# A hybrid token mixer on one core: the first recurrent phase rewritten with channels on partitions

## The chip, the cores and the metric

One core of a Trainium2 chip runs the whole program once. The metric is device time in microseconds (us), from the profiler's first to last event; lower is better. The engines are TensorE (PE, with its weight loads as PEld), VectorE (DVE), ScalarE (ACT), GpSimd (POOL) and SyncE (SP), which issues most DMAs.

## The reference, cut to what matters

Two layers of a mixer over 256 context and 1024 latent tokens of width 1024. Each layer projects the normed tokens and runs four groups of heads: a gated long convolution, a bidirectional RWKV-7 recurrence, windowed attention and dense attention. The change is in the recurrence:

```python
kk = heads(k * k_k); kk = kk / max(norm(kk), 1e-12)
for d in range(2):                       # forward and backward
    w_log = -softplus(-(w0[d] + tanh(w_low) @ w_up[d])) - 0.5
    a = sigmoid(a0[d] + a_low @ a_up[d])
    k_d = k * (1 + (a - 1) * k_a)
    w = exp(-exp(w_log))
# per token: S = S * w + (S @ -kk) (kk * a)^T + v k_d^T ;  y = S @ r
bonus = sum(r * (k_fwd + k_bwd) * r_k) * v
```

There are four heads of 64 channels. The kernel computes the recurrence in chunks of 64 tokens: within a chunk the products of decayed keys, queries and removal vectors form triangular Gram matrices, which are inverted by blocks.

## The kernel before, in words

Everything is fp32; the large projections run as three fp32r products (high and low halves of tokens and weights). Instructions are written in program order, and a planner fixes each engine's queue ahead of time: an instruction goes to its engine when its operands are expected and no earlier one is ready. `nc.any` lets the planner choose VectorE or ScalarE.

**Projections.** `chan` (L240 to L249) computes 128 output channels, in groups of 24 matmuls, into one of three PSUM banks `acc`; `conv` (L251) copies a group into `zp`, which has one buffer, and applies a three-tap convolution (L261 to L263). `attn` (L301) uses the same tag `acc`. `beside` (L284) adds the projections that other stages need; `spread` and `mark` tie each group to a point in TensorE's order, here to the ends of the first eight of ten tiles (PACE_A is 0 to 0.8).

**The first recurrent phase**, `phase_a` (L449), takes ten tiles of 128 tokens. `stage_a` (L481) loads r, k, v and the low-rank rows with channels on partitions (L484 to L489), computes the decays (`p_w`, L491), transposes r, k and v to tokens on partitions (`p_rk`, `p_v`), and forms sigmoid rates, cumulative decays (`p_ex`, `p_in`, L520, triangular fp32r matmuls over high and low halves), the chunk's total decay (`p_wt`, L532), normed keys (L535 to L544), and the operands AL, BK and rho (L546 to L560), all token-major and on VectorE. Then sixteen transposes (L576 to L579) bring them back to channels on partitions as AR and BKT, and sixteen matmuls give the Gram matrices `p_g` (L594), which VectorE masks into GG (L597). Blocks of GG are copied into cL and cN (L607, L610) and stored to `ls_d` and `no_d`; `p_r` (L619) closes the tile, and the mark is set there. Copies by `cpy` all carry line L456.

**The solves.** After tiles 4, 8 and 10, `solve` (L624) loads the 32x32 blocks (L631), copies them into Lx, the upper half reversed, and inverts them in 31 steps of two VectorE operations each (L641, L642); the result is copied (L644) and stored from ScalarE's queue (L645, L646). All its tiles have one buffer.

**After it.** The projections of two more gate blocks are tied behind the last tile; then the long convolution (`hyena`) begins, then the second recurrent phase (`phase_b`), which reads what the first one stored, beside the attentions.

PSUM in this stretch: `acc` 3 banks, tag a 2, tag g 3.

Of the kernel before, what the change touches and what calls it, by code (L numbers as in the profile page):

```python
# [7 lines left out]
F32 = mybir.dt.float32  # L8
F32R = mybir.dt.float32r
# [206 lines left out]
class Proj:  # L216
# [18 lines left out]
    def chan(w, blk, ctx, pace=None):  # L235
# [64 lines left out]
    def attn(w, sa, pq):  # L300
# [20 lines left out]
        for a, blk in ((0, B_WA), (1, B_FA)):  # L321
# [4 lines left out]
            for half in range(2):  # L326
# [8 lines left out]
                for t in (list(range(8)) + ([8, 9] if half or not w.last else [])):  # L335
                    lat = t < 8
                    ps = pp.tile([128, 512], F32, tag="acc", bufs=3, name="acc")
# [73 lines left out]
def rw_consts(c):  # L411
# [6 lines left out]
    c["cind"] = (((s // 64)[:, None] == np.arange(2)[None, :]).astype(f) * f(NE))  # L418
# [7 lines left out]
class Rwkv:  # L426
# [7 lines left out]
    def __init__(w, k, l, keep, dp):  # L434
# [10 lines left out]
        w.ls_d = [T(f"ls_d{i}_", [2, m, 4, 4, 32, 32]) for i, m in enumerate(w.NBAT)]  # L445
# [3 lines left out]
    def phase_a(w, ep, sp, pp):  # L449
# [5 lines left out]
        PT = nc.gpsimd.tensor_tensor  # L455
        cpy = lambda o, i: nc.any.tensor_copy(o, i)  # L456
        vcp = cpy
        ld = lambda n, shape, src: (lambda t: (nc.scalar.dma_start(out=t, in_=src), t)[1])(ep.tile(shape, F32, name=n))
        tri = ep.tile([128, 4, 128], F32R, name="trir")
        t = ep.tile([128, 4, 128], F32, tag="zb", bufs=2, name="tri")  # L460
        nc.scalar.dma_start(out=t, in_=A["tri"])
        nc.any.tensor_copy(tri, t)
        rv = ld("rvec", [128, 3, 256], A["rvec"][l, :, 0:3])
        cind = ld("cind", [128, 2], A["cind"])
        gmask = ld("gmask", [128, 2, 2, 64], A["gmask"])
        wup = ld("wup", [65, 512], A["wup"][l])
        aup = ld("aup", [65, 512], A["aup"][l])
        LW = [ep.tile([65, 2, 128], F32, name=f"LW{i}") for i in range(2)]
        for i in range(2):
            nc.sync.dma_start(out=LW[i][64:65], in_=A["ones"][0:2].rearrange("(o a) c -> o a c", o=1))  # L470
        W2, W1 = 7, 5
        w2 = lambda n, shape=(128, 2, 256): sp.tile(list(shape), F32, tag="w2", bufs=W2, name=n)
        w1 = lambda n, shape=(128, 256): sp.tile(list(shape), F32, tag="w1", bufs=W1, name=n)
        pa = lambda n, shape=(128, 512): pp.tile(list(shape), F32, tag="a", bufs=2, name=n)
        pg_ = lambda n, shape=(128, 512): pp.tile(list(shape), F32, tag="g", bufs=3, name=n)
        d2 = lambda x: x.unsqueeze(1).to_broadcast([128, 2, 256])
        h4 = lambda x: x.rearrange("p (h d) -> p h d", d=64)
        half = lambda c: slice(c * 64, c * 64 + 64)

        def stage_a(b, n):  # L480
            t0 = b * 128  # L481
            zb = ep.tile([128, 8, 128], F32, tag="zb", bufs=2, name="zb")
            q = nc.sync if n else nc.scalar
            q.dma_start(out=zb[:, 0:6, :], in_=k.rw_d[0:768, t0:t0 + 128].rearrange("(c p) t -> p c t", p=128))  # L484
            for c in range(2):
                q.dma_start(out=zb[:, 6:8, half(c)],
                                  in_=k.rw_d[512:768, t0 + (1 - c) * 64:t0 + (2 - c) * 64].rearrange("(c p) t -> p c t", p=128))
            lw = LW[n % 2]
            q.dma_start(out=lw[0:64], in_=k.rw_d[768:896, t0:t0 + 128].rearrange("(c p) t -> p c t", p=64))  # L489
            ps = pa("p_w")  # L490
            nc.tensor.matmul(ps, lw[:, 0, :], wup, start=True, stop=True)  # L491
            sig = w2("sig")
            nc.scalar.activation(sig, ps, AF.Tanh, scale=0.5)
            nc.any.tensor_scalar(sig, sig, 0.5, 0.5, op0=ALU.mult, op1=ALU.add)
            p0 = pa("p_rk", (128, 4, 128))
            for i in range(4):
                nc.tensor.transpose(p0[:, i, :], zb[:, i, :], k.ident)
            rk = w2("rk")
            cpy(rk, p0)
            r_, k_ = rk[:, 0, :], rk[:, 1, :]  # L500
            p1 = pa("p_v", (128, 4, 128))
            for i in range(4):
                nc.tensor.transpose(p1[:, i, :], zb[:, 4 + i, :], k.ident)
# [4 lines left out]
            ps = pa("p_a")  # L508
            nc.tensor.matmul(ps, lw[:, 1, :], aup, start=True, stop=True)
            ta = w2("ta")  # L510
            nc.scalar.activation(ta, ps, AF.Tanh, scale=0.5)
            ss = [sp.tile([128, 2, 256], F32R, tag=f"ss{i}", bufs=1, name=f"ss{i}") for i in range(2)]
            nc.any.tensor_copy(ss[0], sig)
            TT(ss[1], sig, ss[0].bitcast(F32), op=ALU.subtract)
            E = []
            for nm, kinds in (("ex", (0, 2)), ("in", (1, 3))):
                ps = pa("p_" + nm, (128, 2, 256))
                for d in range(2):
                    for i, x in enumerate(ss):
                        nc.tensor.matmul(ps[:, d, :], tri[:, kinds[d], :], x[:, d, :], start=(i == 0), stop=(i == 1))  # L520
                e = w2("e" + nm)
                nc.scalar.activation(e, ps, AF.Exp, scale=NE)
                E.append(e)
                if nm == "in":
                    e = w2("en")
                    nc.scalar.activation(e, ps, AF.Exp, scale=-NE)
                    E.append(e)
            E1, E3, E2 = E
            ps = pa("p_wt", (128, 2, 2, 2))
            for d in range(2):  # L530
                for hp in range(2):
                    nc.tensor.matmul(ps[:, d, :, hp], sig[:, d, hp * 128:(hp + 1) * 128], cind, start=True, stop=True)  # L532
            nc.scalar.activation(w.WT[:, b], ps.rearrange("p d c h -> p (d c h)"), AF.Exp)
            kkr = w1("kkr")
            TT(kkr, k_, rv[:, 0, :], op=ALU.mult)  # L535
            sq = w1("sq")
            nc.scalar.activation(sq, kkr, AF.Square)
            ss = sp.tile([128, 4], F32, tag="ss", bufs=2, name="ss")
            nc.vector.tensor_reduce(ss, h4(sq), axis=AX.X, op=ALU.add)
            nc.vector.tensor_scalar(ss, ss, 1e-24, None, op0=ALU.max)  # L540
            s2 = sp.tile([128, 4], F32, tag="s2", bufs=2, name="s2")
            PT(s2, ss, k.mhalf[:, :4], op=ALU.pow)
            kkh = w1("kkh")
            STT(h4(kkh), h4(kkr), 0.5, s2.unsqueeze(2).to_broadcast([128, 4, 64]), op0=ALU.mult, op1=ALU.mult)  # L544
            AL = sp.tile([128, 2, 2, 256], F32, tag="AL", bufs=2, name="AL")
            STT(AL[:, 0], E1, -2.0, d2(kkh), op0=ALU.mult, op1=ALU.mult)  # L546
            kka = w2("kka")
            STT(kka, ta, 1.0, d2(kkh), op0=ALU.add, op1=ALU.mult)
            kxa = w1("kxa")
            STT(kxa, k_, 0.5, rv[:, 1, :], op0=ALU.mult, op1=ALU.mult)  # L550
            kd = w2("kd")
            STT(kd, ta, -1.0, d2(kxa), op0=ALU.add, op1=ALU.mult)
            TT(kd, kd, d2(k_), op=ALU.add)
            rho = w2("rho")
            BK = sp.tile([128, 2, 2, 256], F32, tag="BK", bufs=2, name="BK")
            for c in range(2):
                q, z = half(c), half(1 - c)
# [1094 lines left out]
```

## Time and profile before

| | |
|---|---|
| three runs, median (lowest, highest) | 2539.47 us (2528.05, 2540.99) |
| the profiled execution, its time | 2539.31 us |
| its span, first to last instruction | 2537.5 us |
| busy: PE, PEld, DVE, ACT, POOL | 2231.6, 1844.7, 1740.8, 1079.7, 270.0 us |
| mean granted TensorE clock | 0.926 of 2.4 GHz |
| DMA | 359.07 MB, mean 142 GB/s |

The busy times overlap; no engine is full over the whole span, and the stages have different limits. A busy TensorE is not a TensorE at its peak, since matmuls are pipelined.

### The profile page before, as it was taken

What the parts mean: (1) busy time and instruction counts of PE and PEld (TensorE: products, weight loads), DVE (VectorE), ACT (ScalarE), POOL (GpSimd) and SP (SyncE); (2) the same over time, 40 slices, a digit from 0 to 9 for tenths busy, and PEclk for the clock granted to TensorE, in tenths of its full rate; (3) what the DMA queues carried; (4) which work ended last, traced back from release to release, by engine and by line L of the source; (5) the groups of instructions that cost most, each with busy time, mean ns of one, the idle gap of its engine ahead of it and who ended that gap; (6) DMA issues with size and microseconds to landing.
All of it is one profiled execution on the core that took longest, in us unless ns stands there. A gap on an engine that the chain in (4) does not pass through costs nothing.

```text
span 2537.5 us, 44541 instructions
## 1 busy us (share of the span) xinstructions
PE 2231.6 (88%) x16864; PEld 1844.7 (73%) x16864; DVE 1740.8 (69%) x4146; ACT 1079.7 (43%) x2564; POOL 270.0 (11%) x404
## 2 busy tenths in 40 slices
PE   6899898998948699999798998989987669999898
PEld 3687677777847577886586887978776557877676
DVE  6985445789778666667543786657997886656753
ACT  5422222544211366766544322335542107766651
POOL 1000221000000001002122001310000000001212
PEclk9899899899778799999998998999987879999999
DMA  8224574556422746443433222444655155563332
GB/s 266 75 102 162 185 229 108 155 171 201 158 86 79 230 117 183 146 144 89 141 124 117 94 90 95 133 125 142 179 177 169 67 137 169 173 202 94 120 129 100
DMA packets 288690, 359.07 MB, mean 142 GB/s; under 512 B 108007, under 2 KB 229910, under 8 KB 283100
## 3 DMA queue, kind: packets, MB, share of 16 engines
q1 hardware_dynamic: 261704, 261.60, 33.3%
q0 software_dynamic: 11232, 70.78, 8.2%
q10 hardware_dynamic: 15540, 23.84, 2.9%
q8 instruction: 133, 2.18, 0.4%
q14 instruction: 81, 0.66, 0.1%
HBM read 227.31 MB, written 128.84 MB: 140 GB/s over the span
## 4 chain that ended last, share of the span: by engine, by line
PE 68%; DVE 11%; DMA 9%; ACT 5%; issue 5%; SPq 1%; POOL 0%; ACTq 0%; POOLq 0%; DVEq 0%
PE acc L246 20%; PE acc L340 9%; PE ops L1112 8%; PE O L1014 3%; PE pt L1004 3%; DMA st_d<-ST 2%; PE p_g L594 2%; PE pk L1326 2%; PE S L973 2%; ACT P L988 1%; PE pr L1387 1%; PE mps L130 1%; PE S L974 1%; PE ph L1302 1%; DVE tmp L641 1%
## 5 line engine op out<-in xcount | busy, mean ns | idle before, releaser
L246 PE MATMUL acc<-hhi,wh 128*128 128x512 f32 (+1 forms) x896 | 219.8, 383 | 7.8 <-ACT wh L232 5.2
L246 PE MATMUL acc<-hlo,wh 128*128 128x512 f32 (+1 forms) x896 | 213.7, 373 | 0.0
L246 PE MATMUL acc<-hhi,wl 128*128 128x512 f32 (+1 forms) x896 | 211.0, 371 | 1.5 <-DVE wl L233 1.5
L978 DVE TENSOR_REDUCE st<-S 128x1 f32<-128x512 f32 (+1 forms) x320 | 172.1, 560 | 55.9 <-PE S L974 40.0
L988 ACT ACTIVATE P<-S,st 128x512 f32<-128x512 f32 (+1 forms) x320 | 183.9, 585 | 24.2 <-DVE st L981 21.7
L246 PEld LDWEIGHTS acc<-hhi,wh 128*128 128x128 f32 x896 | 159.0, 198 | 40.0 <-ACT wh L232 7.2
L246 PEld LDWEIGHTS acc<-hhi,wl 128*128 128x128 f32 x896 | 155.2, 190 | 32.6 <-issue 5.8
L246 PEld LDWEIGHTS acc<-hlo,wh 128*128 128x128 f32 x896 | 157.1, 193 | 28.0 <-issue 2.0
L944 ACT COPY PT<-pt 128x512 f32<-128x512 f32 (+2 forms) x284 | 133.4, 497 | 91.5 <-PE pt L1004 89.7
L1004 PE MATMUL pt<-ident,P 128*128 128x128 f32 x976 | 158.8, 286 | 13.6 <-ACT P L988 6.2
L973 PE MATMUL S<-kp,qs 128*128 128x256 f32 (+2 forms) x384 | 141.4, 377 | 23.8 <-ACT P L988 23.1
L1004 PEld LDWEIGHTS pt<-ident,P 128*128 128x128 f32 x976 | 113.4, 144 | 43.3 <-issue 15.2
L1014 PE MATMUL O<-PT,V 128*64 128x256 f32 x976 | 133.2, 386 | 1.8 <-ACT PT L944 1.8
L974 PE MATMUL S<-kp,qs 128*128 128x256 f32 (+2 forms) x384 | 120.4, 327 | 1.3 <-DMA kp<-qk_d 1.3
L232 ACT ACTIVATE wh<-wr 128x1024 fp32r<-128x1024 f32 x58 | 60.7, 1057 | 116.9 <-PE acc L246 88.6
L973 PEld LDWEIGHTS S<-kp,qs 128*128 128x128 f32 x384 | 75.4, 197 | 42.4 <-ACT P L988 30.8
L1014 PEld LDWEIGHTS O<-PT,V 128*64 128x64 f32 x976 | 70.9, 136 | 42.5 <-issue 5.2
L340 PE MATMUL acc<-wh,hhi 128*128 128x256 f32 x608 | 93.3, 296 | 2.0 <-ACT wh L232 2.0
L258 ACT COPY zp<-acc 128x512 f32<-128x512 f32 (+1 forms) x64 | 33.6, 531 | 143.4 <-PE acc L246 109.1
L340 PE MATMUL acc<-wl,hhi 128*128 128x256 f32 x608 | 90.5, 289 | 4.1 <-POOL wl L233 4.1
L594 PEld LDWEIGHTS p_g<-AR,BKT 64*128 64x128 f32 x640 | 72.0, 209 | 27.1 <-ACT BKT L456 8.8
L345 ACT ACTIVATE qx<-acc 128x256 f32<-128x256 f32 x76 | 29.2, 384 | 137.9 <-PE acc L340 136.7
(397 smaller groups left out, 5290.8 us busy)
## 6 DMA issues: line engine op xcount, KB each, us to landing
IN<-in_d POOLq DMA_DIRECT2D x18, 2048.0 KB, 10.0
wr<-in_w_in POOLq DMA_DIRECT2D x58, 512.0 KB, 4.3
mw<-in_mod_w SPq DMA_DIRECT2D x48, 512.0 KB
in_d<-BK SPq DMA_DIRECT2D x20, 512.0 KB
in_d<-AL SPq DMA_DIRECT2D x20, 512.0 KB
kp<-qk_d SPq DMA_DIRECT2D x32, 320.0 KB
qk_d<-qo SPq DMA_DIRECT2D x72, 128.0 KB
in_d<-GG SPq DMA_DIRECT2D x18, 512.0 KB
```

The lines of the kernel that those rows point to most:

```text
L232: w.k.nc.scalar.activation(h, r, AF.Copy)
L246: nc.tensor.matmul(ps[:, :n], a[:, kc * 128:(kc + 1) * 128], b[:, kc, t0:t0 + n], start=(i == 0 and kc == 0), stop=(i == 2 and kc == 7))
L340: nc.tensor.matmul(ps[:, :256], x_[:, kc, t * 128:(t + 1) * 128], w_[:, kc, :], start=(n == 0 and kc == 0), stop=(n == 2 and kc == 7))
L594: nc.tensor.matmul(pg[:, hp, c], BKT[q, hp, c], AR[q, :, hp, half(c)], start=True, stop=True)
L944: nc.any.tensor_copy(o, i)
L973: nc.tensor.matmul(ps[:, w0:w0 + w], qs[:, hd % 2, hd // 2], kp[kv][0][:, t0:t0 + w], start=True, stop=False)
L974: nc.tensor.matmul(ps[:, w0:w0 + w], qs[:, hd % 2, hd // 2], kp[kv][1][:, t0:t0 + w], start=False, stop=not masks)
L978: TR(ng[:, i:i + 1], ps[:, :w0], axis=AX.X, op=ALU.max, negate=True)
L988: nc.scalar.activation(P[:, :w], ps[:, :w], AF.Exp, bias=gm, accum_out=den[:, i:i + 1])
L1004: nc.tensor.transpose(pt[:, i, :], P[:, i * 128:(i + 1) * 128], k.ident)
L1014: nc.tensor.matmul(O[kv * 64:kv * 64 + 64, 0], V[:, t, kv * 64:kv * 64 + 64], PTs[kv][:, i], start=(i == 0), stop=(i == nt - 1))
L1112: nc.tensor.matmul(ps, a[:, kc, :], b[:, kc, s], start=(n == 0 and kc == 0), stop=(n == 2 and kc == 7))
```

## The change

Work stays with channels on partitions as long as it can. `stage_a` is split in two. `early` loads k, the low-rank rows, r and v, squares the keys and sums them by a matmul with head indicators (`p_n`), computes the decays and rates, forms all cumulative decays at once with channels on partitions (`p_e`: the sigmoid is the stationary operand, the triangular matrices move, in fp32), takes the chunk's total decay out of that result, and spreads the key norms over channels by a matmul with a broadcast operand. `products` forms AR and BKT directly, takes the Gram matrices, stores blocks straight from GG (eight stores instead of three), makes the token-major copies AL and BK by twelve transposes, and computes the bonus sums by matmuls (`p_bon`). `early` of tile n+1 is written ahead of `products` of tile n. The solve loads its blocks tile by tile and direction by direction, without the copy into Lx's lower half. The tag `acc` has two PSUM banks, as `p_n` takes one. The rest of the diff (layout of the constants, one line in `phase_b`) follows from this and is left out.

```diff
-            ps = w.pp.tile([128, 512], F32, tag="acc", bufs=3, name="acc")
+            ps = w.pp.tile([128, 512], F32, tag="acc", bufs=2, name="acc")
...
-        def stage_a(b, n):
+        def early(b, n):
+            t0 = b * 128
             q = nc.sync if n else nc.scalar
+            X = ep.tile([128, 2, 3, 128], F32, tag="X3", bufs=2, name="X3")
+            q.dma_start(out=X[:, :, 0], in_=rows(256, 256, slice(t0, t0 + 128)))
             lw = LW[n % 2]
             q.dma_start(out=lw[0:64], in_=k.rw_d[768:896, t0:t0 + 128].rearrange("(c p) t -> p c t", p=64))
+            q.dma_start(out=X[:, :, 2], in_=rows(0, 256, slice(t0, t0 + 128)))
+            zv = ep.tile([128, 4, 128], F32, tag="zv", bufs=1, name="zv")
+            q.dma_start(out=zv[:, 0:2], in_=rows(512, 256, slice(t0, t0 + 128)))
+            for c in range(2):
+                q.dma_start(out=zv[:, 2:4, half(c)], in_=rows(512, 256, slice(t0 + (1 - c) * 64, t0 + (2 - c) * 64)))
+            for p in range(2):
+                ACT(sq[:, p], X[:, p, 0], AF.Square, scale=rv[:, 0, p:p + 1])
+            pn = pp.tile([128, 3, 128], F32, tag="n", bufs=1, name="p_n")
+            for p in range(2):
+                nc.tensor.matmul(pn[:, 2, 2 * p:2 * p + 2], sq[:, p], ind, start=True, stop=True)
...
+            ACT(ta, ps, AF.Tanh, scale=0.5)
+            KK = w4("KK")
+            nc.any.tensor_scalar(KK[:, :, :, 1].rearrange("q p d t -> q (p d) t"), pd(ta), -0.5, -0.5, op0=ALU.mult, op1=ALU.add)
+            for p in range(2):
+                ACT(KK[:, p, :, 0], ta[:, p], AF.Identity, scale=cf[:, 1, p:p + 1], bias=cf[:, 2, p:p + 1])
...
+            for p in range(2):
+                ps = pa("p_e", (128, 2, 2, 128))
+                for d in range(2):
+                    c0 = d * 256 + p * 128
+                    nc.tensor.matmul(ps[:, d], sig[:, c0:c0 + 128], tri[:, 2 * d:2 * d + 2], start=True, stop=True)
+                ACT(AR[:, p], ps, AF.Exp, scale=NE)
+                ACT(E2[:, p], ps[:, :, 1], AF.Exp, scale=-NE)
...
+            for h in range(4):
+                nc.tensor.matmul(pn[half(h % 2), h // 2], s2[:, h:h + 1].to_broadcast([128, 64]), k.ident, start=True, stop=True)
+            for p in range(2):
+                STT(X[:, p, 1], X[:, p, 0], cf[:, 0, p:p + 1], pn[:, p], op0=ALU.mult, op1=ALU.mult)
+            return X, KK, AR, E2, VV
+
+        def products(b, X, KK, AR, E2, VV):
+            TT(at(KK), at(KK), two(0), op=ALU.mult)
+            BKT = w4("BKT", (128, 2, 2, 2, 2, 64))
+            for c in range(2):
+                x = KK.rearrange("q p d a t -> q (p d) a t")[:, :, :, half(c)]
+                TT(BKT.rearrange("q p d c a t -> q (p d) c a t")[:, :, c], x if c else x[:, :, ::-1],
+                   pd(E2)[:, :, half(c)].unsqueeze(2).to_broadcast([128, 4, 2, 64]), op=ALU.mult)
+            TT(at(AR), at(AR), two(1), op=ALU.mult)
+            if need_y:
...
+                TT(M, KK[:, :, :, 0], X[:, :, 2:3].to_broadcast([128, 2, 2, 128]), op=ALU.mult)
...
             for c in range(2):
                 for hf in range(2):
-                    p = c * 64 + hf * 32
-                    cpy(cL[p:p + 32], Gu[p:p + 32, :, c, hf * 32:hf * 32 + 32])
+                    e = c * 2 + hf
+                    o = slice(32 * e, 32 * e + 32)
+                    nc.sync.dma_start(out=w.ls_d[i][m].rearrange("d u e s t -> e s (d u) t")[e], in_=Gu[o, :, c, hf * 32:hf * 32 + 32])
...
+                    nc.sync.dma_start(out=w.no_d[b][o].rearrange("p (u t) -> p u t", t=32), in_=Gu[o, 4 * d:4 * d + 4, c, x:x + 32])
...
+                for p in range(2):
+                    for d in range(2):
+                        nc.tensor.matmul(ps[:, 2 * p:2 * p + 2], M[:, p, d], rki[:, p], start=(d == 0), stop=(d == 1))
+                cpy(w.bon[:, b, :], ps)
...
-            nc.sync.dma_start(out=Ld[:P], in_=flat(w.ls_d[i]))
...
-            cpy(Lx[lo], Ld[lo])
+            for m in range(w.NBAT[i]):
+                for d, t in ((1, Ld), (0, Lx)):
+                    o = 16 * (d * w.NBAT[i] + m)
+                    nc.sync.dma_start(out=t[o:o + 16].rearrange("p s t -> p (s t)"), in_=rows(w.ls_d[i], d)[m])
...
+        nxt = early(w.ORDER[0], 0)
         for n, b in enumerate(w.ORDER):
-            stage_a(b, n)
+            cur = nxt
+            if n < 9:
+                nxt = early(w.ORDER[n + 1], n + 1)
+            products(b, *cur)
             if n in (3, 7, 9):
                 solve(n // 4)
             yield
```

## Rows read from the trace of the kernel before

**Rows 1.** Busy time by stretch, both layers (window, length, engines, granted clock, DMA share).

```profile
468.10:624.20 156.10, 152.47 (x1122) 125.41 (x1120) 136.92 (x287) 74.45 (x147) 10.89 (x20) 1.00 0.59 175
624.20:664.10 39.90, 30.14 (x206) 25.25 (x200) 36.38 (x86) 15.07 (x33) 1.01 (x1) 0.64 0.41 121
664.10:717.00 52.90, 33.60 (x190) 29.50 (x188) 38.18 (x104) 8.29 (x15) 1.12 (x2) 0.82 0.58 191
...
1730.80:1875.20 144.40, 142.40 (x1004) 113.59 (x1000) 129.23 (x272) 73.79 (x146) 9.61 (x19) 0.98 0.57 173
1875.20:1917.00 41.80, 30.70 (x204) 24.51 (x199) 39.40 (x97) 14.26 (x31) 2.03 (x2) 0.66 0.41 124
```

**Rows 2.** Waits, 664 to 717 us: who waited for whom, total, times, longest.

```profile
ACT u L1372 <- DVE XR L644: 17.5, 1, 17.5
```

**Rows 3.** Groups of VectorE instructions, 434.5 to 666.5 us: busy and mean ns, idle before.

```profile
L559 DVE TENSOR_TENSOR BK<-kd,en 64x512 f32<-64x512 f32 x20 | 13.7, 686 | 0.6
...
L233 DVE TENSOR_TENSOR wl<-wr,wh 128x1024 fp32r<-128x1024 f32 x6 | 7.3, 1219 | 0.1
L553 DVE TENSOR_TENSOR kd<-kd,rk 128x512 f32<-128x512 f32 x10 | 6.9, 689 | 0.2
...
L456 DVE COPY cN<-GG 32x128 f32<-32x128 f32 x22 | 4.9, 221 | 0.5
...
L564 DVE TENSOR_TENSOR bs<-kd 128x256 f32<-128x256 f32 x10 | 4.3, 426 | 0.3
```

**Rows 4.** Chain of waits at full clock, 1740 to 1800 us (start, us, what).

```profile
1746.31 0.67 PE p_ex L520 x4
1746.98 0.47 PE p_in L520 x4
...
1752.48 0.79 PE p_wt L532 x8
...
1753.44 0.86 PE p_w L491 x2
...
1758.04 0.44 PE p_rk L497 x4
```

**Rows 5.** Timeline of the first tile of layer 0 (start, length, engine, line).

```profile
435.38 5.03 ACTq L486 DMA_DIRECT2D zb<-rw_d  x2
...
440.45 0.65 ACTq L489 DMA_DIRECT2D LW<-rw_d  x1
...
445.08 2.07 PE L491 MATMUL p_w<-wup,LW 65*128 65x512 f32 x2 [9.62 <-DMA LW<-rw_d]
...
460.83 2.60 PE L594 MATMUL p_g<-AR,BKT 64*128 64x128 f32 x24
```

**Rows 6.** Busy time, pairs of tiles in layer 1 with equal projection work.

```profile
1730.80:1770.70 39.90, 39.73 (x296) 32.14 (x292) 29.96 (x56) 20.75 (x43) 2.83 (x7) 1.00 0.43 139
1770.70:1815.80 45.10, 43.68 (x304) 34.24 (x301) 41.02 (x85) 25.21 (x49) 3.54 (x8) 0.97 0.64 192
...
1833.90:1875.20 41.30, 41.14 (x297) 32.91 (x292) 40.42 (x94) 20.42 (x41) 3.22 (x4) 1.00 0.65 196
```

**Rows 7.** VectorE timeline, 618 to 722 us: the second and third solve.

```profile
633.42 0.69 DVE L634 COPY Lx<-Ld 64x1024 f32<-64x1024 f32 x1 [2.18 <-DMA Ld<-ls_d]
...
677.62 0.69 DVE L644 COPY XR<-X 64x1024 f32<-64x1024 f32 x1
...
690.26 0.18 DVE L641 TENSOR_TENSOR tmp<-Lx,X 64x31 f32<-64x31 f32 x1 [0.40 <-ACT Lx L456]
...
715.31 0.68 DVE L644 COPY XR<-X 32x1024 f32<-32x1024 f32 x1
```

**Rows 8.** Timeline of the rw projections of layer 0, 173 us.

```profile
173.28 2.10 PE L246 MATMUL acc<-hhi,wh 128*128 128x512 f32 x8
...
173.37 0.86 ACT L258 COPY zp<-acc 128x256 f32<-128x256 f32 x2 [6.33 <-PE acc L246]
```

**Rows 9.** Instructions on ls_d, whole span: duration ns min/median/max, first and last start.

```profile
L612 SPq DMA_DIRECT2D ls_d<-cL x40: 373/530/1822, 471.0 to 1919.2; - x40
```

More of the change, by code (lines that the diff above doesn't have):

```diff
@@ L483, in stage_a @@
             q = nc.sync if n else nc.scalar
[L484 to L487, printed above, removed]
+            rows = lambda r, m, s: k.rw_d[r:r + m, s].rearrange("(c p) t -> p c t", p=128)
+            X = ep.tile([128, 2, 3, 128], F32, tag="X3", bufs=2, name="X3")
@@ L496, in stage_a @@
[L496 to L500, printed above, removed]
+            ps = pa("p_a", (128, 2, 2, 128))
+            for p in range(2):
+                for d in range(2):
+                    c0 = d * 256 + p * 128
+                    nc.tensor.matmul(ps[:, p, d], aup[:, c0:c0 + 128], lw[:, 1, :], start=True, stop=True)
+            ta = w2("ta")
+            ACT(ta, ps, AF.Tanh, scale=0.5)
@@ L528, in stage_a @@
[L528 to L555, printed above, removed]
@@ L556, in stage_a @@
-            for c in range(2):
-                q, z = half(c), half(1 - c)
-                TT(BK[q, c], kka[q], E2[q], op=ALU.mult)
-                TT(BK[z, c], kd[q], E2[q], op=ALU.mult)
-            TT(rho, E3, d2(r_), op=ALU.mult)
-            nc.sync.dma_start(out=w.bk_d[b], in_=BK)
-            if not (last and b >= 8):
-                bs = w1("bs")
-                TT(bs, kd[:, 0, :], kd[:, 1, :], op=ALU.add)
-                TT(bs, bs, r_, op=ALU.mult)
-                TT(bs, bs, rv[:, 2, :], op=ALU.mult)
-                nc.vector.tensor_reduce(w.bon[:, b, :], h4(bs), axis=AX.X, op=ALU.add)
+            AR = w4("AR")
@@ L568, in stage_a @@
             GG = sp.tile([128, 2, 2, 2, 2, 2, 64], F32, tag="GG", bufs=1, name="GG")
             GA, GR = GG[:, :, :, :, :, 0], GG[:, :, :, :, :, 1]
-            ops = []
             for d in range(2):
-                p0 = pg_("p_ar", (128, 2, 2, 128))
-                p1 = pg_("p_bk", (128, 2, 2, 128))
-                for hp in range(2):
-                    sl = slice(hp * 128, hp * 128 + 128)
-                    nc.tensor.transpose(p0[:, 0, hp, :], AL[:, 0, d, sl], k.ident)
-                    nc.tensor.transpose(p0[:, 1, hp, :], rho[:, d, sl], k.ident)
-                    for c in range(2):
-                        nc.tensor.transpose(p1[:, hp, c, :], BK[:, c, d, sl], k.ident)
-                AR = w2("AR", (128, 2, 2, 128))
-                cpy(AR, p0)
-                if not (last and b >= 8):
-                    nc.sync.dma_start(out=w.rh_d[b][:, 256 * d:256 * d + 256], in_=AR[:, 1])
-                BKT = w2("BKT", (128, 2, 2, 128))
-                cpy(BKT, p1)
-                ops.append((AR, BKT))
@@ L587, in stage_a @@
-            for d in range(2):
-                AR, BKT = ops[d]
                 for par in range(2):
                     pg = pg_("p_g", (128, 2, 2, 2, 64))
-                    q = half(par)
-                    for hp in range(2):
+                    o = half(par)
+                    for p in range(2):
                         for c in range(2):
-                            nc.tensor.matmul(pg[:, hp, c], BKT[q, hp, c], AR[q, :, hp, half(c)], start=True, stop=True)
-                    z = 1 if last and b >= 8 else 2
+                            nc.tensor.matmul(pg[:, p, c], BKT[o, p, d, c], AR[o, p, d, :, half(c)], start=True, stop=True)
@@ new lines, in products @@
+            AL = sp.tile([128, 2, 2, 256], F32, tag="o4", bufs=2, name="AL")
+            p0 = pg_("p_al", (128, 2, 2, 128))
+            for d in range(2):
+                for p in range(2):
+                    nc.tensor.transpose(p0[:, d, p], AR[:, p, d, 0], k.ident)
+            cpy(AL[:, 0], p0.rearrange("t d p e -> t d (p e)"))
+            BK = sp.tile([128, 2, 2, 256], F32, tag="o4", bufs=2, name="BK")
+            for c in range(2):
+                p0 = pg_("p_bk", (128, 2, 2, 128))
+                for d in range(2):
+                    for p in range(2):
+                        nc.tensor.transpose(p0[:, d, p], BKT[:, p, d, c].rearrange("q a t -> q (a t)"), k.ident)
+                cpy(BK[:, c], p0.rearrange("t d p e -> t d (p e)"))
@@ L614, in stage_a @@
+            nc.sync.dma_start(out=w.bk_d[b], in_=BK)
+            if need_y:
+                ps = pg_("p_bon", (128, 4))
+                for p in range(2):
+                    for d in range(2):
+                        nc.tensor.matmul(ps[:, 2 * p:2 * p + 2], M[:, p, d], rki[:, p], start=(d == 0), stop=(d == 1))
+                cpy(w.bon[:, b, :], ps)
             pr = pg_("p_r", (128, 2, 4, 64))
```

99 lines of the change are left out of this document (46 added, 53 removed).

## The prediction, made blind

> **What bounds the kernel now.** I read the busy time by stretch first, then the chain of waits, then the groups of instructions inside the phase, and last the timelines of its two ends. The change touches the first recurrent phase of each layer: about 230 us in layer 0 (434 to 664 us) and 220 us in layer 1 (1698 to 1917 us), 18% of the 2537.5 us span together.
>
> In its body, from the last matmul of the first token tile to that of the eighth, TensorE is busy 152.5 of 156.1 us at the full granted clock, 2.4 GHz, and VectorE 136.9 us; in layer 1 142.4 and 129.2 of 144.4 us [rows 1]. Both engines are nearly full, because the other projections are fed in between. In the tail (the last two tiles) no projection is left: VectorE is busy 36.4 of 39.9 us and 39.4 of 41.8 us, TensorE 30 us, at a mean granted clock of 0.64 and 0.66, so between its two levels [rows 1]. The tail is VectorE's, since the second 32x32 solve runs there beside the tiles. Then a third solve, VectorE alone, must finish before the long convolution starts: ScalarE waits 17.5 us for its last copy [rows 2]. So three things set the start of the next stage: the first tile's latency, TensorE in the body, and VectorE's tile work mixed into the second solve.
>
> Durations come from the profiled execution, 2539.31 us for a span of 2537.5 us; the median of the three runs shown is 2539.47 us, so the sum can be set against either.
>
> **Part 1, VectorE and ScalarE.** With channels on partitions, per-channel factors become scalars of an instruction, and products with r, k and the keys run once for both directions. Gone per tile from VectorE: six operations on 512 elements (low half of the sigmoid, kka, AL, two on kd, rho) at 0.69 us, four 64-partition products at 0.686 us, eight operations of 256 elements at 0.42 us, and VectorE's share of the copies into cL and cN, some 1.0 us a tile [rows 3]: 4.1 + 2.7 + 3.4 + 1.0 = 11.2 us. Added: two products of 1024 elements at 1.22 us, three of 512 at 0.69 us (two for BKT, one for M) and two of 128 elements, which I put at 0.3 us each, under the 0.42 us of 256 elements [rows 3]: 5.1 us. Net 6 us less per tile. ScalarE loses casts and copies and gains two exponentials of 256 elements; it is busy 74 of 156 us [rows 1], so I cost it at nothing. If that cover went, 2 us a tile would show.
>
> **Part 2, TensorE.** At the full clock a 512-column fp32 matmul of two weight halves costs 0.86 us, a two-column one 0.79/4 = 0.20 us, a transpose 0.11 us, and the eight fp32r matmuls of the cumulative sums 1.14 us [rows 4]. Added per tile: the cumulative sums as four fp32 matmuls of 256 columns, 4 x 0.43 = 1.72 us; two norm sums, 0.40 us; four broadcasts of 128 columns, 4 x 0.215 = 0.86 us; four bonus sums, 0.79 us. Gone: 1.14 us, the decay sums 0.79 us, four r and k transposes 0.44 us, four of the eight AL and rho transposes 0.44 us. Net +0.96 us. Over the eight tiles up to the tail that is **+8 us** a layer if TensorE is the limit. Here the row (busy 98%) speaks for the whole price; the lower end is 0. I take 8.
>
> The Trainium skill, page "Trainium Kernel Development and Optimization", section "Performance Expectations", calls matmul busy time a bad measure because matmuls are pipelined, and goes by weight-load busy time. That is 125.4 of 156.1 us, 80% [rows 1]; by it there is slack and the term would be 0, the whole sum 16 us lower. The sum keeps the row on busy time, because the pair of tiles in which VectorE is only 75% busy is no shorter than TensorE's busy time in it, 39.73 of 39.9 us [rows 6].
>
> **Part 3, relief in the body.** In layer 1 pairs of tiles with equal projection work take 39.9 us before the first solve starts (VectorE 30 us) and 45.1 and 41.3 us with it (VectorE 41 and 40.4 us) [rows 6]. The excess, 5.2 and 1.4 us, with room for one more pair, is what VectorE can be charged with: between 0 and 8 us a layer, and part of it coincides with a dip of the clock (0.97). I take **-5 us** a layer.
>
> **Part 4, the first tile.** TensorE waits 9.6 us for LW, whose load sits behind two loads that hold ScalarE's queue for 5.0 us [rows 5]. The change puts it second; the halves of v follow it. That is worth up to 4.5 us here, less in layer 1. From p_w to p_g there are 15.75 us at the low clock [rows 5]; the new chain (two more exponentials, three products instead of ten) would be some 5 us shorter, but the second tile's early stage now stands before the first tile's products and takes TensorE meanwhile. Between -9.5 and 0, I take **-4 us** a layer.
>
> **Part 5, the tail.** The second solve takes from 633.4 to 677.6 us, 44.2 us, where the third one, alone, takes 25.1 us [rows 7]: 19 us of tile work sit between its 62 steps. Two tiles shed 12 us of VectorE work, and VectorE is 93% busy there, so **-11 us** a layer; bounds 0 (steps bound by latency) and -18.
>
> **Part 6, DMAs.** Per tile SP issues 13 transfers now and 20 after: two more loads, two more ls_d and three more no_d stores. At a median of 0.53 us [rows 9] that is 3.7 us of a 20 us tile, hidden as SP issues some 7 us a tile now. Each solve's load becomes eight (four for the last) on SP, with waits for the solve before in front of them; the copy into Lx's lower half goes. I charge **+1 us** a layer, 0 to 3. GG has one buffer and is now held by nine stores instead of copies; see the rivals.
>
> **Part 7, two accumulator banks instead of three.** Where zp is still in use, a finished group holds a bank. At 173.28 us a new group starts while ScalarE copies two older groups until 174.2 us [rows 8]: with two banks it would wait about half a us for the first of them. Three more such places, in layer 1, cost 0.4 to 1.0 us. **+3 us** in all; lower end 0, upper end one 0.59 us copy for each of 26 convolved blocks, 15 us.
>
> **Part 8, two stages in the source.** The order of the queues already mixes tiles: p_w and p_rk of one tile (1753 and 1758 us) directly follow the decay sums of the tile before it, whose products are still to come [rows 4]. So this alone I put at 0; what it may cost at the first tile is in part 4.
>
> Sum: 2 x (8 - 5 - 4 - 11 + 1) + 3 = -19 us, **2520 us**.
>
> **Rivals.** *TensorE is the bound to the end, slower.* If the tail too becomes TensorE's (its 30 us of 39.9 at a reduced clock [rows 1] grow, and early stages run ahead of the products a solve waits for), VectorE's relief buys nothing: 20 x 0.96 + 3 = +22 us, 2561 us. It decides once TensorE is over 95% busy in the last two tiles. Against it: 10 us idle there now.
>
> *The solve or GG holds the pace, no change.* If the steps are latency-bound, or the masks and GG's nine stores (4 x 0.69 + 9 x 0.53 = 7.5 us and the landing) fill the 20 us of a tile, for which an issue must take up to 1.9 us where the longest now is 1.8 us [rows 9], the tail keeps its length: -19 + 22 = +3 us, 2542 us. The Trainium skill, page "DMA: Bandwidth & Descriptors", section "Specifications", has transfers under 512 B done as read-modify-write below line rate, which would push this way, since no_d goes from 512 B rows to 128 B; no row here separates the two sizes.
>
> *More than forecast.* TensorE has the slack and the tail loses all 18 us: 2 x (0 - 5 - 4 - 18 + 1) + 3 = -49 us, 2490 us.
>
> *The order does not follow the source.* As part 8 has it, this moves nothing in the sum.
>
> **How the numbers follow.** Forecast 0.42, more than forecast 0.16, no change 0.25, TensorE to the end 0.17. Run to run this kernel can be told from no change at about 0.5%, 12.7 us, so faster means under 2526.8 us. The forecast's own range is 2504 to 2534 us: three quarters of it count as faster, with nearly all of the larger gain and little of the rest: 0.32 + 0.16 + 0.04 = 0.52. Same takes a quarter of the forecast and most of no change, 0.30; slower 0.18. The range 2486 to 2552 us leaves out the far half of the slower case and the end of the faster one.
>
> **What would show it.** Right: VectorE's busy time between first and last tile falls by some 60 us a layer, the second solve takes about 33 instead of 44 us, the long convolution starts some 11 us earlier in layer 0 and 19 us in layer 1, and the stages after it keep their length. Wrong: tiles of the body over 21 us with TensorE full; SP issues over 1.5 us and VectorE waiting before the masks; or TensorE waiting for acc in the projections.

## The result and the profile after

The changed kernel takes 2493.18 us, the median of four runs (2491.84 to 2497.09); the kernel before, run beside it, 2533.76 us (2524.45 to 2540.99). The ratio is 0.9844, 95% interval 0.9804 to 0.9885: 1.6% or some 40 us faster, where 19 us were forecast. The profiled execution took 2493.41 us for a span of 2491.6 us, 45.9 us less than the span before. From the first p_w to the next attention the time fell from 403.3 to 389.4 us in layer 0 and from 385.6 to 368.2 us in layer 1, 31 of these 46 us. The first p_w came 5 us (layer 0) and 4 us (layer 1) earlier in its stage; the other 5 us lie in stages that the change hardly touches. Gains below are worked out from the ratios, times 2535 us for the kernel before, whose median ran from 2533.8 to 2540.6 us on the chips used.

Busy time by stretch of the changed kernel (window, length, then PE, PEld, DVE, ACT and POOL busy with their instructions, granted clock, DMA share, GB/s), layer 0 and then layer 1, each in the order body, last two tiles, from there to the third solve's last copy:

```profile
468.40:586.70 118.30, 115.76 (x953) 95.60 (x947) 79.98 (x167) 55.34 (x122) 8.59 (x12) 0.99 0.66 189
586.70:627.60 40.90, 38.51 (x302) 32.95 (x296) 33.19 (x63) 13.97 (x25) 1.32 (x6) 0.96 0.59 168
627.60:688.40 60.80, 57.56 (x303) 49.41 (x298) 41.02 (x106) 11.15 (x17) 2.12 (x4) 0.97 0.52 177
1704.70:1827.90 123.20, 121.72 (x942) 99.20 (x938) 85.56 (x176) 57.47 (x122) 9.82 (x17) 0.94 0.62 181
1827.90:1866.60 38.70, 38.70 (x281) 32.14 (x278) 30.86 (x65) 11.62 (x21) 1.11 (x2) 1.00 0.63 189
1866.60:1913.50 46.90, 34.77 (x166) 28.54 (x162) 36.64 (x99) 7.36 (x10) 1.59 (x3) 0.90 0.68 231
```

Against [rows 1] three things stand out. The body lost 38 and 21 us. The tail is as long as it was (40.9 for 39.9 us, 38.7 for 41.8), but TensorE is now busy through it and its clock is near 2.4 GHz instead of between the two levels (0.96 and 1.00 for 0.64 and 0.66). And in layer 0 the stretch of the third solve grew to 60.8 us, with TensorE busy 57.6 of them, where before it was 51.2 us to the same copy with TensorE busy 33.6 (the row of [rows 1] runs on to 717 us). In layer 1 it grew less, from 43.3 to 46.9 us, and TensorE still idles 12 us of it. The projections' matmuls alone show why, for layer 0, first before, then after:

```profile
468.10:624.20 156.10, 81.16 (x360) 58.97 (x360) 1.00 0.59 175
624.20:664.10 39.90, 0.00 (x0) 0.00 (x0) 0.64 0.41 121
664.10:717.00 52.90, 31.57 (x168) 27.58 (x168) 0.82 0.58 191
```

```profile
468.40:586.70 118.30, 34.72 (x133) 21.92 (x133) 0.99 0.66 189
586.70:627.60 40.90, 24.48 (x110) 18.30 (x110) 0.96 0.59 168
627.60:688.40 60.80, 56.53 (x285) 48.24 (x285) 0.97 0.52 177
```

Of the 360 that ran in the body, 133 are left there; 110 run in the tail and 117 more beside the third solve. The edit itself doesn't move them: their due times are the same. In layer 1, 120 of 240 left the body, 98 for the tail and 22 for the third solve.

What ScalarE waits for at the start of the long convolution tells who ends the phase. Before it was the solve's last copy, 17.5 us in layer 0 [rows 2] and 13.7 us in layer 1. After, in layer 0, ScalarE waits 1.6 us, by the profile for TensorE's matmul; the solve's copy (L638) ends at 689.08 us, 0.4 us before ScalarE goes on, so that the two end together. In layer 1 it is still the solve, with 14.2 us (last line):

```profile
598.75 0.69 DVE L628 COPY Lx<-Ld 64x1024 f32<-64x1024 f32 x1 [6.18 <-DMA Ld<-ls_d]
...
641.22 0.69 DVE L638 COPY XR<-X 64x1024 f32<-64x1024 f32 x1
...
688.40 0.68 DVE L638 COPY XR<-X 32x1024 f32<-32x1024 f32 x1
...
689.47 1.07 ACT L1372 COPY u<-pd 128x512 f32<-128x512 f32 x2 [1.56 <-PE pd L1371]
...
1914.63 1.07 ACT L1372 COPY u<-pd 128x512 f32<-128x512 f32 x2 [14.21 <-DVE XR L638]
```

The second solve takes 42.5 us (598.75 to 641.22) for 44.2 [rows 7].

### The profile page after: what moved, and what is told of

It is laid out like the page before. It is cut to its first block, busy times and chain, and to the rows that moved or that the text cites. A ratio compares the mean times of both kernels' runs of the same rounds, so it can differ in the third digit from the quotient of the medians.

```text
span 2491.6 us, 44786 instructions
## 1 busy us (share of the span) xinstructions
PE 2223.9 (89%) x17048; PEld 1843.7 (74%) x17048; DVE 1632.7 (66%) x3880; ACT 1056.9 (42%) x2536; POOL 272.4 (11%) x404
## 4 chain that ended last, share of the span: by engine, by line
PE 67%; DMA 11%; DVE 10%; issue 5%; ACT 5%; SPq 1%; POOL 0%; ACTq 0%; POOLq 0%; DVEq 0%
PE acc L246 16%; PE acc L340 9%; PE ops L1112 8%; PE O L1014 3%; PE pt L1004 3%; PE p_g L570 2%; PE S L973 2%; DMA st_d<-ST 2%; PE pk L1326 2%; PE S L974 2%; PE pr L1387 1%; PE mps L130 1%; PE p_e L533 1%; ACT P L988 1%; PE ph L1302 1%
## 5 line engine op out<-in xcount | busy, mean ns | idle before, releaser
L973 PE MATMUL S<-kp,qs 128*128 128x256 f32 (+2 forms) x384 | 142.5, 379 | 17.5 <-ACT P L988 17.0
L232 ACT ACTIVATE wh<-wr 128x1024 fp32r<-128x1024 f32 x58 | 60.8, 1058 | 105.3 <-PE acc L246 93.3
L340 PE MATMUL acc<-wh,hlo 128*128 128x256 f32 x608 | 87.3, 285 | 0.0
```

The costliest lines, as they stand in the source:

```text
L232: w.k.nc.scalar.activation(h, r, AF.Copy)
L340: nc.tensor.matmul(ps[:, :256], x_[:, kc, t * 128:(t + 1) * 128], w_[:, kc, :], start=(n == 0 and kc == 0), stop=(n == 2 and kc == 7))
L973: nc.tensor.matmul(ps[:, w0:w0 + w], qs[:, hd % 2, hd // 2], kp[kv][0][:, t0:t0 + w], start=True, stop=False)
```

## The experiments

Theory: VectorE's relief made the gain, and TensorE's dearer work was paid in full. Rivals: the look-ahead in the source, the place of the projections, or slack on TensorE. Each kernel ran with the kernel before on the same chip.

**Relief taken back, all tiles.** In the changed kernel:

```diff
-                TT(M, KK[:, :, :, 0], X[:, :, 2:3].to_broadcast([128, 2, 2, 128]), op=ALU.mult)
+                for _ in range(10):
+                    TT(M, KK[:, :, :, 0], X[:, :, 2:3].to_broadcast([128, 2, 2, 128]), op=ALU.mult)
```

> The changed kernel with M formed ten times over in each tile that forms it: nine more VectorE products of 512 elements at 0.68 us, 6.1 us a tile, which is what the change took from VectorE; TensorE's work, the DMAs and the order stay. If VectorE's relief is what emptied TensorE's waits in the tail and in the third solve, nearly all of the gain is given back: +25 to +40 us on the changed kernel's 2493, so 2518 to 2533, the second solve longer by some 12 us, and TensorE's share of the last two tiles back under 85%. If instead the look-ahead in the source or the place of the projections gave the gain, VectorE has the room and the time moves by 0 to +10 us.

Measured 2552.64 us, ratio 1.0061 (1.0045 to 1.0078): slower than before, and 55 us behind the changed kernel, more than the whole gain. VectorE's load matters, more than expected here; and with that load in place the change is a loss of 15 us, about the price of its dearer TensorE work (16 us, below). The nine added products stand in one block in the source, where the work taken away was spread over the tile. The expected fall of TensorE's share in the last two tiles did not come in layer 0 (34.43 of 34.43 us). There the time went into the body, 148.9 for 118.3 us; TensorE was busy 143.6 of them at a granted clock of 0.83, so part of it is the lower clock. In layer 1 it went mostly into the stretch of the third solve (last line), 75.8 for 46.7 us, where ScalarE waits 46.2 us for the solve's last copy:

```profile
475.91:624.84 148.93, 143.61 (x1002) 121.46 (x1002) 119.02 (x220) 57.28 (x127) 12.27 (x17) 0.83 0.52 152
624.84:659.27 34.43, 34.43 (x274) 29.31 (x274) 30.56 (x60) 9.92 (x18) 1.60 (x2) 1.00 0.62 183
659.27:723.10 63.83, 47.83 (x262) 41.51 (x262) 50.19 (x131) 9.38 (x15) 2.11 (x4) 0.91 0.56 191
...
1898.15:1973.91 75.76, 32.17 (x137) 26.15 (x136) 49.61 (x136) 5.11 (x7) 1.05 (x2) 0.70 0.49 153
```

**Relief taken back, last two tiles only.**

```diff
+                for _ in range(10 if b in (3, 4) else 1):
```

> The changed kernel with M formed ten times in the last two tiles of each layer only (12.3 us more of VectorE's work a layer, beside the second solve). The forecast's step put 11 us a layer on these two tiles and 5 on the other eight: by it +22 us, 2515, more than a third of the 59 us that the same addition to all tiles cost. If the relief is shared by the tiles alike, 2 of 9 tiles: +13 us. If it was nearly all in the body, 0 to +5 us.

Measured 2498.53 us, ratio 0.9854 (0.9829 to 0.9879): 3 us by the ratios, 5 by the medians. By the time, 24 us of VectorE work in the tails of the changed kernel cost little. In layer 0 the two tiles got longer (48.41 us for 40.9) and the stretch after them shorter (56.06 for 60.8), as more projections ran in the tail (161 of their matmuls for 110) and fewer behind it; from the first p_w to the next attention it took 389.7 us for 389.4. In layer 1, where the solve ends the phase, the same took 377.3 us for 368.2: 9 of the 12 us show there, and stages that no edit touched were 5 us shorter in this profile. So the work was free in layer 0 alone.

**Relief alone.** In the kernel before, with VectorE's work left out. What it computes is no longer the mixer, so it serves for its time alone (the factor 0.001 keeps the stand-in small):

```diff
-            STT(kka, ta, 1.0, d2(kkh), op0=ALU.add, op1=ALU.mult)
...
-            STT(kxa, k_, 0.5, rv[:, 1, :], op0=ALU.mult, op1=ALU.mult)
...
-            STT(kd, ta, -1.0, d2(kxa), op0=ALU.add, op1=ALU.mult)
-            TT(kd, kd, d2(k_), op=ALU.add)
-            rho = w2("rho")
+            rho = E3
...
-                TT(BK[q, c], kka[q], E2[q], op=ALU.mult)
-                TT(BK[z, c], kd[q], E2[q], op=ALU.mult)
-            TT(rho, E3, d2(r_), op=ALU.mult)
+                STT(BK[:, c], E2, 0.001, ta, op0=ALU.mult, op1=ALU.mult)
...
-                TT(bs, kd[:, 0, :], kd[:, 1, :], op=ALU.add)
-                TT(bs, bs, r_, op=ALU.mult)
-                TT(bs, bs, rv[:, 2, :], op=ALU.mult)
-                nc.vector.tensor_reduce(w.bon[:, b, :], h4(bs), axis=AX.X, op=ALU.add)
+                nc.vector.tensor_reduce(w.bon[:, b, :], h4(r_), axis=AX.X, op=ALU.add)
```

> The kernel before with work left out on VectorE alone: no kka, kd, kxa and rho (the tanh and the exponential stand in for them), two products for BK over 128 partitions instead of four over 64, and no three products for the bonus; by the rows 5.8 us less a tile, 113 us in all. TensorE's work, the layout, the DMAs and the due times stay. If VectorE's load is what the change relieved, this alone gives all of that gain without the changed kernel's dearer TensorE work: -45 to -65 us on the kernel before, so 2473 to 2493, at or below the changed kernel. If the channel layout, the DMAs or the order gave the gain, -15 us or less.

Measured 2501.38 us, ratio 0.9857 (0.9837 to 0.9877): -36 us, neither theory's number. The relief is the largest part, but not all of it: the changed kernel is no slower, with 16 us more of TensorE's work. The stretches tell what is left, the body, tail and third solve of layer 0, then the tail and third solve of layer 1:

```profile
466.41:617.97 151.56, 151.56 (x1109) 124.26 (x1109) 97.31 (x208) 78.62 (x155) 9.96 (x19) 1.00 0.59 174
617.97:642.13 24.16, 21.67 (x205) 18.12 (x205) 20.58 (x49) 14.37 (x32) 1.92 (x2) 0.93 0.76 238
642.13:698.36 56.23, 34.30 (x185) 29.91 (x184) 44.54 (x120) 7.72 (x13) 1.11 (x2) 0.82 0.55 177
...
1845.92:1869.27 23.35, 20.17 (x198) 16.54 (x197) 19.87 (x51) 13.57 (x30) 1.01 (x1) 0.99 0.70 205
1869.27:1926.33 57.06, 32.62 (x136) 26.74 (x136) 43.12 (x116) 7.25 (x11) 1.12 (x2) 0.77 0.52 169
```

Here the tail does shrink, from 39.9 to 24.2 us in layer 0 and from 41.8 to 23.4 us in layer 1, and in layer 0's body TensorE is busy without a gap. But the stretch of the third solve got 5 and 14 us longer: TensorE idles 22 of 56 and 24 of 57 us there, and ScalarE waits 24 us for the solve's last copy in either layer. From the first p_w to the third solve's end it is 15 us (layer 0) and 12 us (layer 1) less, 27 of the 36 us.

**Due times alone, and with the relief.** `PACE_A` of the kernel before set to (0.0, 1.0), first by itself, then on top of the relief:

> The kernel before with only the projections' due times spread over the whole of the first recurrent phase (0 to 1.0 instead of 0 to 0.8), so that some of them fall into the last two tiles, as they do in the changed kernel. If it is the place of the projections alone that closed TensorE's waits there, some 20 us less than the kernel before (2514 of 2534). If VectorE's work bounds the tail whatever TensorE is given, little: -8 to +8 us, with the body shorter and the tail longer by about the same.

Measured 2541.14 us, ratio 1.0026 (1.0007 to 1.0045), 7 us slower: with VectorE full, 73 matmuls of the projections in layer 0's tail and 49 in layer 1's buy nothing.

> The kernel before with VectorE's work left out as in before_less_vector (kka, kd, kxa, rho, two of the BK products, three of the bonus) and the due times spread over the whole phase (0 to 1.0). The relief alone gave 34 us, the due times alone -4. If the two work together (with VectorE relieved, the tail and the third solve have room that only projections can fill), 10 to 20 us less than the relief alone: 2481 to 2491, below the changed kernel. If the place of the projections is worth nothing, 2496 to 2506.

Measured 2504.80 us, ratio 0.9877 (0.9849 to 0.9906): no better than the relief alone. These due times end at the last tile, so no more of the projections came beside the third solve (168 matmuls in layer 0, as before), where the room was. That was the fault of the experiment, and the next one mends it.

**Relief, and projections beside the third solve.** The same kernel with `PACE_A` (0.0, 1.4).

> before_less_vector with the due times spread over 0 to 1.4 of the phase, so that the last 28% of the projections stand behind the tiles and run beside the third solve, as they do in the changed kernel. There TensorE idled 22 us (of 56) with the relief alone, 3 us (of 61) in the changed kernel's layer 0. If this overlap is the rest of the changed kernel's gain, 10 to 20 us less than the relief alone, 2481 to 2491, with the phase to the third solve's end shorter by as much and the long convolution's stage no longer. If the place is worth nothing, 2496 to 2508, the third solve or the long convolution's stage growing by what the body loses.

Measured 2485.25 us, ratio 0.9778 (0.9756 to 0.9800), -56 us: 20 us more than the relief alone by the ratios, 15 us by the two profiles. The phase to the third solve's end fell from 255.2 to 247.3 us in layer 0 and from 240.9 to 232.2 us in layer 1, TensorE's idle time beside the solve from 22 to 5 us in layer 0 and from 24 to 12 us in layer 1, and ScalarE's wait for the solve's copy from 24 to 5 and 14 us. The long convolution's stage grew by 4 us in layer 0, so that 13 us are left where the projections moved. The stretches of layer 0:

```profile
464.76:595.93 131.17, 128.23 (x974) 104.60 (x973) 93.29 (x201) 72.00 (x148) 9.68 (x22) 0.97 0.64 190
595.93:630.98 35.05, 32.81 (x270) 27.86 (x269) 27.89 (x63) 17.23 (x35) 1.65 (x2) 1.00 0.55 169
630.98:689.21 58.23, 53.27 (x281) 45.98 (x280) 43.99 (x117) 12.03 (x19) 2.17 (x4) 0.97 0.60 196
```

**TensorE's price.** In the changed kernel:

```diff
-                for d in range(2):
+                for d in (0, 1, 0, 1):
                     c0 = d * 256 + p * 128
                     nc.tensor.matmul(ps[:, d], sig[:, c0:c0 + 128], tri[:, 2 * d:2 * d + 2], start=True, stop=True)
```

> The changed kernel with the four matmuls of the cumulative sums issued twice: 1.72 us more TensorE work a tile at 2.4 GHz, 34 us over the 20 tiles. If TensorE now sets the length of the phase from its first tile to the third solve, nearly all of it shows: +20 to +34 us, 2513 to 2527. If the phase has slack on TensorE, as a price of 0 for the added matmuls would have it, 0 to +10 us.

Measured 2524.38 us, ratio 0.9958 (0.9939 to 0.9977), 29 us behind the changed kernel by the ratios: 0.84 us for each us of TensorE's work. There is next to no slack.

**The look-ahead.** In the changed kernel:

```diff
-        nxt = early(w.ORDER[0], 0)
         for n, b in enumerate(w.ORDER):
-            cur = nxt
-            if n < 9:
-                nxt = early(w.ORDER[n + 1], n + 1)
+            cur = early(b, n)
             products(b, *cur)
```

> The changed kernel with the early stage of a tile put directly before its own products instead of before the products of the tile ahead of it; all work stays. If the gain is VectorE's relief, 0 to +8 us on 2493 (the queues mixed tiles before as well, and the first tile gets rid of the second one's early stage). If the look-ahead carried the gain, +20 to +40 us: the kernel falls back to 2513 to 2533, with TensorE idle again in the last two tiles.

Measured 2489.46 us, ratio 0.9815 (0.9782 to 0.9847): not slower, perhaps some us faster. The pipelining in the source carries none of the gain. It does shift the projections: layer 0's phase is 12 us shorter than in the changed kernel, and the long convolution's stage 13 us longer, with 371 of the projections' matmuls in it instead of 264.

**Due times of the changed kernel.** `PACE_A` set to (0.0, 0.5).

> The changed kernel with the projections' due times in the first half of the phase (0 to 0.5 instead of 0 to 0.8). In its profile 244 to 395 of the projections' matmuls run in the tail and beside the third solve, where the kernel before has none to 168. If that place is part of the gain (matmuls that fill the time in which VectorE solves alone), drawing them forward costs: +6 to +18 us on 2493, with fewer of them behind the eighth tile and TensorE idle again beside the third solve. If only VectorE's work counts, or if the due times do not hold the projections where they are, -5 to +5 us.

Measured 2495.29 us, ratio 0.9841 (0.9813 to 0.9870): no difference. The projections alone show that in layer 0 they stayed beside the solve, 264 of them for 285:

```profile
472.66:599.41 126.75, 36.91 (x121) 22.12 (x121) 0.92 0.62 176
599.41:637.29 37.88, 24.68 (x120) 19.22 (x120) 1.00 0.69 205
637.29:692.86 55.57, 51.77 (x264) 44.21 (x264) 0.97 0.51 179
```

So the due times, which only say how early a group may run, don't hold them there. That the planner puts the tiles' matmuls first because their operands are now expected sooner is what fits, but no run shows it; and what their place is worth in the changed kernel itself stays untested.

**Accumulator banks.** In the kernel before:

```diff
-            ps = w.pp.tile([128, 512], F32, tag="acc", bufs=3, name="acc")
+            ps = w.pp.tile([128, 512], F32, tag="acc", bufs=2, name="acc")
```

at both places of the tag.

> The kernel before with two accumulator banks instead of three in the projections and at the place of the attention that shares them; nothing else. The forecast's part 7: +3 us, bounds 0 and +15. A rival: the projections behind the convolved blocks wait at every block, +10 to +15 us, so that the change gave away that much.

Measured 2538.67 us, ratio 1.0004 (0.9986 to 1.0022): +1 us, nothing that can be told from zero.

**A version that beats both.** The changed kernel without the look-ahead, and with

```diff
+            hi = sp.tile([128, 512], F32R, tag="sh", bufs=1, name="sh")
+            nc.scalar.copy(hi, sig)
+            lo = sp.tile([128, 512], F32R, tag="sl", bufs=1, name="sl")
+            nc.gpsimd.tensor_tensor(lo, sig, hi.bitcast(F32), op=ALU.subtract)
...
-                    nc.tensor.matmul(ps[:, d], sig[:, c0:c0 + 128], tri[:, 2 * d:2 * d + 2], start=True, stop=True)
+                    for i, x in enumerate((hi, lo)):
+                        nc.tensor.matmul(ps[:, d], x[:, c0:c0 + 128], tri[:, 2 * d:2 * d + 2], start=(i == 0), stop=(i == 1))
...
-                M = w2("M")
-                TT(M, KK[:, :, :, 0], X[:, :, 2:3].to_broadcast([128, 2, 2, 128]), op=ALU.mult)
+                M = KK[:, :, :, 0]
+                nc.gpsimd.tensor_tensor(M, KK[:, :, :, 0], X[:, :, 2:3].to_broadcast([128, 2, 2, 128]), op=ALU.mult)
+                nc.gpsimd.tensor_tensor(M[:, :, 0], M[:, :, 0], M[:, :, 1], op=ALU.add)
...
-                    for d in range(2):
-                        nc.tensor.matmul(ps[:, 2 * p:2 * p + 2], M[:, p, d], rki[:, p], start=(d == 0), stop=(d == 1))
+                    nc.tensor.matmul(ps[:, 2 * p:2 * p + 2], M[:, p, 0], rki[:, p], start=True, stop=True)
```

(the table `tri` is rounded to fp32r as in the kernel before, and the tag w2 has three buffers).

> The changed kernel without the look-ahead, with the decay sums as eight fp32r matmuls on a high and a low half (1.14 us instead of 1.72 us of TensorE a tile; the halves formed by ScalarE and GpSimd) and with the bonus product and the sum of its two directions on GpSimd (0.68 us of VectorE and 0.40 us of TensorE less a tile). By the prices of the two runs before (31 us for 34 us of TensorE's work, 59 us for 110 us of VectorE's): 0.98 us x 20 x 0.9 = 18 us and 12 us x 0.53 = 6 us less than 2489, so 2460 to 2475. If the longer chain to the exponentials (a copy and a GpSimd product of 1.3 us in front of the sums) decides instead, 0 to +10 us on 2489.

Measured 2476.08 us, ratio 0.9766 (0.9739 to 0.9793), 20 us less than the changed kernel by the ratios, and the intervals don't overlap. Against the run without the look-ahead it is 12 us, half of the 24 expected, and how the split and GpSimd share them no run shows. A small variant of it was to repair its first tile:

```diff
-        nc.scalar.dma_start(out=t, in_=A["tri"])
+        nc.sync.dma_start(out=t, in_=A["tri"])
...
-            nc.gpsimd.tensor_tensor(lo, sig, hi.bitcast(F32), op=ALU.subtract)
+            (nc.gpsimd if n else nc.vector).tensor_tensor(lo, sig, hi.bitcast(F32), op=ALU.subtract)
```

> The run with the split decay sums, whose first tile took 34.5 and 29.3 us from p_w to p_r where without the split it took 27.4 and 23.4, with the first tile's low half on VectorE instead of GpSimd and the table of the sums loaded on SP's queue. If the halves' chain is what delays the first tile, -3 to -8 us on 2476; if it is the clock of that stretch (0.50 and 0.62), 0 to -2.

Measured 2497.77 us, ratio 0.9853 (0.9827 to 0.9880): 22 us worse, where both theories had 0 or less. The first tile was no shorter (36.8 us for 34.5), but that is not the loss. The projections' matmuls in the long convolution's stage of layer 0, of the better kernel and of its variant, show one more group of blocks left over for it, and that stage 14 us longer:

```profile
692.16:830.02 137.86, 53.50 (x264) 44.43 (x264) 0.83 0.34 110
```

```profile
685.78:837.65 151.87, 72.79 (x371) 60.87 (x369) 0.87 0.35 109
```

The group alone is not the loss: the run without the look-ahead has the same 371 matmuls there and took 2489 us. In layer 1 the difference is 4 us, and no such group accounts for it. The two profiles are 15 us apart, so part of the loss and its cause stay open.

## Why the prediction was right, and where it was not

The sign and the range held, the size did not: 19 us were forecast, 40 came. Nor did the place: 22 us were to come out of the tails, which nearly kept their length, and the time left the body (38 and 21 us). The forecast's own range, 2504 to 2534 us, misses the result; the wider one covers it because the rival "more than forecast" had stretched it to 2486 us, and that rival's reason did not hold either. Its terms against the runs:

**VectorE's relief (parts 1, 3 and 5): right in size, when it comes alone.** Forecast 5 us a layer in the body and 11 in the tail, 32 us in all; alone in the kernel before it gave 36, of which 27 lie in the two phases. There the body got 4.5 and 5.6 us shorter, as forecast, and the tail 15.8 and 18.5 us, but 5 and 14 of these came back beside the third solve: 10.5 and 4.5 us are left of 11 a layer. In the changed kernel the tail got 1 us longer in layer 0 and 3 us shorter in layer 1. VectorE's busy time from the first p_w to the third solve's end fell from 228.0 to 174.0 us in layer 0 and from 218.0 to 169.0 us in layer 1, somewhat less than the 60 us named.

**TensorE's added work (part 2): right, as far as timed.** 16 us forecast; at the measured 0.84 us for each us, the forecast's own 0.96 us x 20 tiles make +16. That net of 0.96 us was not timed as a whole. In the chain of waits half of a tile's new sums takes 0.86 us, so a tile's 1.72, as put down:

```profile
1755.62 0.86 PE p_e L533 x4
```

The Trainium skill's rule, page "Trainium Kernel Development and Optimization", section "Performance Expectations", would have made this term nothing. With weight loads busy 95.6 of 118.3 us in the changed body, the doubled sums still cost 29 of 34 us, so here busy matmul time was the better guide.

**The first tile (part 4): wrong, and small.** The load moved up did start p_w earlier (a wait of 4.3 us for LW instead of 9.6 [rows 5] in layer 0, of 7.5 instead of 11.6 in layer 1):

```profile
439.92 2.08 PE L506 MATMUL p_w<-wup,LW 65*128 65x512 f32 x2 [4.27 <-DMA LW<-rw_d]
```

But the first tile then took 28.7 instead of 23.3 us, and ended at 468.7 us where it had ended at 468.3; in layer 1 it took 25.7 for 23.4. The chain that was to be some 5 us shorter was longer. The second tile's early stage, named as the risk, explains layer 1, where the run without the look-ahead took 23.4 us again, and not layer 0, where that run still took 27.4. Of the 8 us of this part 2 came, in layer 1.

**DMAs and banks (parts 6 and 7): right to be small.** The banks cost 1 us of the 3, with an interval of -4 to +6 us. The wait for the second solve's load grew from 2.2 [rows 7] to 6.2 us in layer 0; what that cost no run shows. An issue of no_d takes 0.56 us and VectorE waited 1.9 us in all for it:

```profile
L585 SPq DMA_DIRECT2D no_d<-GG x80: 555/559/1917, 461.5 to 1868.5; - x80
...
  DVE GG L573: 1.9, 2
```

**What failed is what the sum took for granted between parts 5 and 8:** that the order of the queues moves nothing, and so that the tail and the third solve keep TensorE's idle time. As to the two stages in the source, part 8 was right (the run without the look-ahead). But what the planner made of the changed work did move: 227 of the projections' matmuls left layer 0's body for those places. In the kernel before, with the relief, such a move was worth 13 us by the profiles' stages and 20 us by the ratios. An account of -36 - 20 + 16 + 1 = -39 us comes near the 40 measured; but it adds runs on different kernels, and no run shows that the parts add up. Three signs named for a right forecast failed although the time fell: the second solve took 42 and not 33 us, with 11 us of the projections' vector work in place of the tiles', the start of the long convolution, by ScalarE's first copy, came 27 us earlier in layer 0 (716.4 to 689.5 us) and not 11, and its own stage, which was to keep its length, gave 8 of them back.

**The rivals.** "TensorE is the bound to the end" came true in its condition in layer 1 and nearly so in layer 0 (100% and 94% busy in the last two tiles, where 95% was named), and false in its price: TensorE became full there by taking over work that had stood in the body, not only by dearer tiles. "More than forecast" had nearly the time, 2490 us, for another reason: TensorE had next to no slack. "The solve or GG holds the pace" is false of GG. The tail did nearly keep its length, but with projections in it. At the end of layer 1's phase the solve does hold the pace still, 14.2 us for 13.7.

## What to carry to other kernels

When two engines are both near full and filler work is fed between them, ask where the filler will go once one of them is relieved: here TensorE idled 31 of 270 us of layer 0's phase before, 24 of 255 with the relief alone and 10 of 247 with projections beside the solve, and that last step brought about half as much again as the relief itself. Price dearer work on the full engine at nearly its busy time, and test a relief both ways, the work taken away alone in the old kernel and put back in the new one: 36 and 55 us, and neither is the answer by itself. Where a planner orders the queues, a change of two lines can shift a whole group across a stage (that stage was 14 us longer here), so compare the place of the filler before the code.

## What was not expected of the hardware

TensorE got more work in layer 0's tail, and its clock rose with it: 0.64 of 2.4 GHz with TensorE idle for 10 of 39.9 us [rows 1], 0.96 with 2.4 of 40.9 us idle, in the same two tiles. And most of layer 0's second recurrent phase with its attentions, up to the output projection, where the change only alters the load of one constant, took 319.1 us in the profile before at a granted clock of 0.97 and 312.4 us in the changed kernel at 0.98, with the same 3536 matmuls. Without the look-ahead it took 304.3 us at 1.00, in another order, with 18 of the matmuls left for later. So single profiles differ by some us in stages that an edit leaves alone, and a gain is placed with care.
